# Attention's written order set by a count of TensorE's own columns instead of a count of calls

## The chip, the cores and the metric

The kernel runs on one core of one Trainium2 chip. The metric is the device time of one execution in microseconds (us), and a kernel's time is the median over its runs.

## What is computed

One inference step of a hybrid decoder layer, for a prompt of 1024 tokens and for 8 sample sequences of 4 tokens each, with a past of 8192 tokens in a paged cache. In the reference, cut to what matters here:

```python
h = rmsnorm(x, g_norm1) * (1 + scale1) + shift1      # shift, scale, gate = silu(c) @ w_ada + b_ada
za, zq, zkv, zg, zm = jnp.split(h @ w_in, SPLIT_IDX, axis=-1)
ya = chunk_spatial_gating(u, vn, w_spatial, b_spatial)
o = g[:, :, 0] * o_cmp + g[:, :, 1] * o_sel + g[:, :, 2] * o_win      # compressed, selected, window
mixed = (gate_a * (ya @ w_branch_a) + gate_b * (yb @ w_branch_b)) @ w_out
x = x + gate1 * mixed
x = x + gate2 * ((gelu(a) * gv) @ w_down)             # a, gv: causal convolution of h2 @ w_up
```

Attention has three branches per query: compressed blocks of 64 keys, a choice of 16 such blocks, and a window of 512 keys. For the prompt 16 blocks are all there are, so the choice takes everything; for the samples the kernel reads all selected-branch pages and masks those not chosen.

## The kernel before, in words

Activations lie transposed, features on the partitions and 1056 columns (1024 prompt, 32 sample) beside them. The stages follow each other: projections and compression of the paged cache, attention (about 612 to 1008 us of the span), the two branch products, the output product, the two feed-forward products.

In the attention three kinds of work share the engines:

- 32 **attention units** of the prompt: 8 tiles of 128 queries, in the order TILES, by 4 pairs of heads (`units`). `scores` puts a unit's products into PSUM, VectorE takes the negative maximum (L1134) and ScalarE the exponentials (L1135). `turn` transposes the probabilities on TensorE (L1160) and copies them back (L1164); `norm` and `values` finish the unit. `step(n)` writes the scores of unit n beside the transposes of unit n-1 and the values of unit n-2.
- 32 **sample units**: 8 sequences by 4 quarters of their pages. `sel_scores(m)` loads 16 pages of 128 KB (psel, issued by `load_pages` on SP's queue: a register load at L512 for every four pages, the DMAs at L522), multiplies them with the queries, adds the mask (L980) and takes the exponentials (L983). `sel_turn` transposes these (L990, copied back at L991); `sel_values` multiplies them with the pages' values (its copy is L1009). `sel_step(m)` writes the values of unit m-1 and then the scores of unit m, 33 steps in all.
- **Chains** of short steps with waits between them, Python generators in `pending`: `qtile` (a tile's compressed branch), `blocks`, `sel_merge` (joins four sample units), `near_turning` and `near_values` (window branch of the samples), `ada_late` (eight loads of w_ada, 2 MB each, L1052, and their products), `turning` (which calls `sel_turn`).

TensorE's order in this stage is the order in which the code writes its instructions (`manual_schedule` for PE); the other engines' order is made by a scheduler. The code decides in two ways. `due` gives for each unit n how many sample steps are to be written by its end, in proportion to the units' work (`work`), and `step` spreads those over its rounds (`at`). And `one_more`, called once or twice a round, lowers each chain's counter by one and runs a chain's next piece when the counter reaches 0: `later(turning(), 3)` is due at the third call. Where a piece is needed and has not been written, `sel_step` and `step` call `one_more` until it has.

The pages go through four buffers in turn (`page_buffer`): sample pages, window loads, w_ada loads, and at the end `ya` and `w_ba` (`ya_load`, L1261 and L1266). A load may start when the buffer's use four loads earlier is over, and the queue issues in order. Behind the attention `branch_a` multiplies `ya`, which `ya_split` splits into two parts, with `w_ba`.

Of the kernel before, what the change touches and what calls it, by code (L numbers as in the profile page):

```python
# [20 lines left out]
NEG = -1e30  # L21
AHEAD = 2
S2, S3 = 4, 2
EARLY = 8
# [26 lines left out]
def step_kernel(tc, A):  # L51
    nc = tc.nc
    sync, act, dve, pool, pe = nc.sync, nc.scalar, nc.vector, nc.gpsimd, nc.tensor

    def mm(out, lhsT, rhs, start, stop):
        return pe.matmul(out, lhsT, rhs, start=start, stop=stop)  # L56

    def behind(ins):
# [693 lines left out]
    def blocks(gr, bank):  # L752
# [21 lines left out]
        dve.tensor_scalar(p, p, r, None, op0=OP.mult)  # L774
        yield 3
        pt = bank()
# [19 lines left out]
        act.copy(pct, pt[:, 0:128])  # L796
        yield 6
        pt = bank()
# [9 lines left out]
        dve.tensor_scalar(oc, po[:, 0:128], GR[:, gr, 0:1], None, op0=OP.mult)  # L808
        yield 2
        pt = bank()  # L810
# [119 lines left out]
    def near_turn(gr):  # L930
        use, wv, s = near[gr]
        pst = R3([128, 640], F32, "pst", 2)
        pt = pM()
        for k in range(4):
            pe.transpose(pt[:, 128 * k:128 * k + 128], s[:, 128 * k:128 * k + 128], ident)
        act.copy(pst[:, 0:512], pt)
        pt = pM()
        pe.transpose(pt[0:32, 0:128], s[:, 512:544], ident)
        pool.memset(pst[:, 512:640], 0.0)
        dve.tensor_copy(pst[0:32, 512:640], pt[0:32, 0:128])  # L940
        near[gr] = use, wv, pst

    def near_values(gr):
        use, wv, pst = near.pop(gr)
        po = pM()
        for k in range(4):
            for i in range(4):
                mm(po[32 * i:32 * i + 32, 0:128], pst[:, 128 * k + 32 * i:128 * k + 32 * i + 32], wv[:, i, k], k == 0, False)
        for i in range(4):
            mm(po[32 * i:32 * i + 32, 0:128], pst[:, 512 + 32 * i:544 + 32 * i], vs_new[:, 128:256], False, True)  # L950
        ow = R3([128, 128], F32, "ou", 7)
        uses[use] = act.copy(ow, po[:, 0:128])
        yield 2
# [32 lines left out]
    def sel_turn(n, s):  # L986
        pst = R3([128, 640], F32, "pst", 2)
        pt = pM()
        for k in range(4):
            pe.transpose(pt[:, 128 * k:128 * k + 128], s[:, 128 * k:128 * k + 128], ident)  # L990
        dve.tensor_copy(pst[:, 0:512], pt)  # L991
        if n % 4 == 0:
            pt = pM()
            pe.transpose(pt[0:32, 0:128], s[:, 512:544], ident)
# [17 lines left out]
    def sel_merge(b):  # L1012
# [5 lines left out]
        dve.tensor_scalar(n4, cg4, nl, None, op0=OP.mult)  # L1018
        yield 3
        pt = pM()  # L1020
# [8 lines left out]
        dve.tensor_reduce(su, sf, axis=AX.X, op=OP.add)  # L1029
        yield 5  # L1030
        pt = pM()
# [6 lines left out]
        for i in range(1, 4):  # L1038
            dve.scalar_tensor_tensor(o, outs[i], f[:, i:i + 1], o, op0=OP.mult, op1=OP.add)
        yield 5  # L1040
        pt = pM()
# [22 lines left out]
    def qtile(i):  # L1064

        tile_of[i] = [q_first if i == TILES[0] else queries(i, KL[1][0]), None]
        yield 1
        c0 = 128 * i
# [18 lines left out]
        dve.tensor_tensor(s, s, z[:, :, None].to_broadcast([128, 8, 16]), op=OP.mult)  # L1087
        yield 8
        pt = pM()
        pe.transpose(pt[:, 0:128], s.rearrange("p a n -> p (a n)"), ident)  # L1090
        ct = R3([128, 128], F32, "ct", 2)
# [55 lines left out]
    def turn(n):  # L1147
# [6 lines left out]
        def group(parts):  # L1154

            pt = pM()
            c = 0
            for branch, h, k, w in parts:
                for b in range(k, k + w):
                    pe.transpose(pt[:, c:c + 128], probs[branch, h][:, 128 * b:128 * b + 128], ident)  # L1160
# [33 lines left out]
    def values(n):  # L1194
# [4 lines left out]
        for branch in range(2):  # L1199
            pe.transpose(pf[:, 128 * branch:128 * branch + 128], f[:, 128 * branch:128 * branch + 128], ident)  # L1200
        fs = R3([128, 256], F32, "fs", 2)
# [15 lines left out]
    def later(steps, wait):  # L1217

        pending.append([wait, steps])

    def one_more():

        for p in list(pending):
            p[0] -= 1
            if p[0] <= 0:
                wait = next(p[1], None)
                if wait is None:
                    pending.remove(p)
                else:
                    p[0] = wait  # L1230

    held, turned = {}, {}

    def sel_step(m):

        if m:
            while m - 1 not in turned:
                one_more()
            use, st, _ = held.pop(m - 1)
            sel_values(m - 1, use, st, turned.pop(m - 1))  # L1240
            if m % 4 == 0:
                later(sel_merge(m // 4 - 1), 2)
        if m < 32:
# [35 lines left out]
    def step(n):  # L1279

        nonlocal m, wba
        ds, gs = attend(n), turn(n - 1)
        if n % 4 == 2 and n + 2 < len(units):
            later(qtile(units[n + 2][0]), 1)
        if ds:
            ds.pop(0)()
        one_more()
        if n >= 2:
            while tile_of[units[n - 2][0]][1] is None:
                one_more()  # L1290
            values(n - 2)
        if gs:
            norm(n - 1)
        mine = list(range(m, due[n]))
        m = max(m, due[n])
        if n in (2, 6):
            near_scores(n // 4)
            later(near_turning(n // 4), 3)
# [5 lines left out]
        assert len(at) == len(mine)  # L1304
        if n % 4 == 1 and n < 32:
            later(ada_late(), 2)
        if n >= len(units):
            for j in range(4)[2 * (n - len(units)):2 * (n - len(units)) + 2]:
                ya_split(j)
        for r in range(rounds):  # L1310
            if r in at:
                sel_step(at[r])
            for _ in range(2):
                if gs:
                    gs.pop(0)()
            one_more()
            if ds:
                ds.pop(0)()
                one_more()
        if n == 0:  # L1320
            later(blocks(1, pM), 1)
        if n == len(units) - 1:
# [3 lines left out]
    with tc.manual_schedule(engines={mybir.EngineType.PE}):  # L1326
        later(qtile(TILES[0]), 0)
        one_more()
        for n in range(len(units) + AHEAD):
            step(n)  # L1330
        ma = []

# [16 lines left out]
        while pending:  # L1349
            one_more()  # L1350
    psum.release()
# [518 lines left out]
```

## Time and profile before

| | |
|---|---|
| median of 3 runs | 1973.37 us (1971.01 to 1976.99) |
| profiled execution | 1970.11 us, span 1968.4 us |
| PE busy | 1853.3 us, 94% of the span |
| PEld (weight loads) busy | 1744.9 us, 89% |
| DVE busy | 1178.6 us, 60% |
| ACT busy | 791.3 us, 40% |
| POOL busy | 486.7 us, 25% |
| moved by DMA | 345.09 MB, mean 175 GB/s |

The profile is of one execution; times in it are from the span's start. PE is TensorE's matmuls, PEld its weight loads, DVE VectorE, ACT ScalarE, POOL GpSimd, SP the engine that issues most DMAs; SPq is its queue. A wait row names the waiting instruction's line, what ended the wait, the total in us, how often, and the longest. In a timeline row the square brackets hold the idle time ahead and what ended it. Almost all matmuls have one line, L56, that of the helper `mm`, so they are told apart by their shapes and neighbours.

### The profile page before, as it was taken

What the parts mean: (1) busy time and instruction counts of PE and PEld (TensorE: products, weight loads), DVE (VectorE), ACT (ScalarE), POOL (GpSimd) and SP (SyncE); (2) the same over time, 40 slices, a digit from 0 to 9 for tenths busy, and PEclk for the clock granted to TensorE, in tenths of its full rate; (3) what the DMA queues carried; (4) which work ended last, traced back from release to release, by engine and by line L of the source; (5) the groups of instructions that cost most, each with busy time, mean ns of one, the idle gap of its engine ahead of it and who ended that gap; (6) DMA issues with size and microseconds to landing.
All of it is one profiled execution on the core that took longest, in us unless ns stands there. A gap on an engine that the chain in (4) does not pass through costs nothing.

```text
span 1968.4 us, 43754 instructions
## 1 busy us (share of the span) xinstructions
PE 1853.3 (94%) x16073; PEld 1744.9 (89%) x16073; DVE 1178.6 (60%) x2532; ACT 791.3 (40%) x1606; POOL 486.7 (25%) x624
## 2 busy tenths in 40 slices
PE   6799999999999998988999999799999999999996
PEld 4799999999997776767679999799999999999996
DVE  5713421112116666675565678899999999756464
ACT  4313111212115554655642366333444444545342
POOL 2510110000001000000002412756867765201010
PEclk9799999999999998999999999899999999999998
DMA  9274656776657777776774454233322223866463
GB/s 328 87 218 126 188 184 211 235 229 208 201 178 247 243 225 233 225 227 218 231 253 154 141 166 135 81 102 107 109 89 72 74 87 95 291 190 211 136 190 89
DMA packets 253607, 345.09 MB, mean 175 GB/s; under 512 B 35249, under 2 KB 189265, under 8 KB 251217
## 3 DMA queue, kind: packets, MB, share of 16 engines
q1 hardware_dynamic: 205408, 261.86, 42.4%
q10 hardware_dynamic: 36896, 41.22, 6.7%
q0 software_dynamic: 11088, 39.21, 5.6%
q8 instruction: 127, 2.08, 0.4%
q14 instruction: 88, 0.71, 0.1%
HBM read 304.91 MB, written 41.43 MB: 176 GB/s over the span
## 4 chain that ended last, share of the span: by engine, by line
PE 80%; DVE 5%; DMA 5%; SPq 4%; issue 3%; ACT 3%; POOL 1%; DVEq 0%; ACTq 0%; POOLq 0%
PE t L56 77%; SPq L522 3%; DMA t<-w_ada 2%; PE t L1160 2%; DVE t L320 1%; DMA t<-t 1%; DMA t<-psel 1%; POOL t L1553 1%; ACT t L319 1%; PE t L990 1%; DVE t L1590 1%; DVE t L1134 0%; SPq L512 0%; DVE t L338 0%; ACT t L1135 0%
## 5 line engine op out<-in xcount | busy, mean ns | idle before, releaser
L56 PE MATMUL t<-t,t 128*128 128x264 f32 (+12 forms) x15298 | 1775.9, 305 | 85.1 <-DVE t L173 14.8
L56 PEld LDWEIGHTS t<-t,t 128*128 128x128 f32 (+3 forms) x15138 | 1661.6, 170 | 135.8 <-issue 51.4
L320 DVE TENSOR_TENSOR t<-t,t 128x512 fp32r<-128x512 f32 (+2 forms) x478 | 386.4, 816 | 320.0 <-ACT t L319 315.9
L319 ACT CAST t<-t 128x512 fp32r<-128x512 f32 (+5 forms) x544 | 311.1, 589 | 440.7 <-PE t L56 342.6
L1590 DVE TENSOR_TENSOR t<-t,t 128x264 f32<-128x264 f32 (+2 forms) x366 | 107.2, 339 | 12.4 <-PE t L56 12.3
L1160 PEld LDWEIGHTS t<-t,t 128*128 128x128 f32 x528 | 58.5, 145 | 32.2 <-issue 13.3
L1191 POOL COPY t<-t 128x256 f32<-128x256 f32 x32 | 13.0, 407 | 279.8 <-DVE t L1189 176.9
L1528 ACT ACTIVATE t<-t,t 128x1072 f32<-128x1072 f32 x44 | 56.6, 1286 | 57.0 <-DVE t L1590 38.2
L1164 ACT COPY t<-t 128x512 f32<-128x512 f32 (+1 forms) x112 | 58.7, 569 | 49.0 <-PE t L1160 48.8
L683 ACT ACTIVATE t<-t 128x384 f32<-128x384 f32 (+1 forms) x48 | 22.2, 465 | 135.8 <-PE t L56 79.6
L1529 DVE SCALAR_TENSOR_TENSOR t<-t,t,t 128x1072 f32<-128x1072 f32 x44 | 73.1, 1661 | 5.0 <-ACT t L1528 4.5
L1160 PE MATMUL t<-t,t 128*128 128x128 f32 x528 | 75.2, 282 | 0.7 <-DVE t L1212 0.3
L1713 POOL TENSOR_TENSOR t<-t,t 128x384 f32<-128x384 f32 (+1 forms) x12 | 14.9, 1275 | 227.9 <-ACT t L1771 227.9
L1135 ACT ACTIVATE t<-t,t 128x640 f32<-128x640 f32 (+3 forms) x64 | 56.1, 877 | 35.7 <-DVE t L1134 31.1
L1530 DVE SCALAR_TENSOR_TENSOR t<-t,t,t 128x1072 f32<-128x1072 f32 x44 | 69.7, 1585 | 0.0
L1553 POOL TENSOR_TENSOR t<-t,t 128x512 f32<-128x512 f32 x22 | 46.6, 2117 | 89.6 <-DMA t<-w_up 79.0
L685 POOL DMA_DIRECT2D t<-t x16 | 8.5, 533 | 241.6 <-DVE t L684 186.8
L1134 DVE TENSOR_REDUCE t<-t 128x1 f32<-128x640 f32 (+3 forms) x64 | 58.9, 921 | 15.3 <-PE t L56 13.9
L1615 POOL TENSOR_TENSOR t<-t,t 128x1024 f32<-128x1024 f32 x22 | 53.8, 2446 | 17.1 <-ACT t L1614 17.1
L980 DVE TENSOR_TENSOR t<-t,t 128x512 f32<-128x512 f32 x32 | 22.1, 691 | 45.0 <-PE t L56 44.9
L1409 POOL TENSOR_TENSOR t<-t,t 128x384 f32<-128x384 f32 (+1 forms) x24 | 28.0, 1168 | 69.2 <-DVE t L1408 66.0
L320 DVE TENSOR_TENSOR t<-t 128x384 fp32r<-128x384 f32 (+1 forms) x66 | 37.0, 586 | 12.9 <-ACT t L319 12.8
(282 smaller groups left out, 1280.3 us busy)
## 6 DMA issues: line engine op xcount, KB each, us to landing
t<-psel SPq DMA_DIRECT2D x512, 128.0 KB
t<-pcmp SPq DMA_DIRECT2D x332, 128.0 KB
t<-w_down SPq DMA_DIRECT2D x120, 256.0 KB
t<-t POOLq DMA_DIRECT2D x50, 528.0 KB, 4.5
t<-w_up SPq DMA_DIRECT2D x96, 256.0 KB
t<-pcmp ACTq DMA_DIRECT2D x180, 128.0 KB
t<-w_ada SPq DMA_DIRECT2D x16, 1024.0 KB
t<-w_t ACTq DMA_DIRECT2D x52, 256.0 KB
```

Of the source, the lines that this page charges most:

```text
L56: return pe.matmul(out, lhsT, rhs, start=start, stop=stop)
L319: act.copy(hi, t)
L320: dve.tensor_tensor(lo, t, hi.bitcast(F32), op=OP.subtract)
L522: d = queue.dma_start(dst, src[bass.ds(r, 1)].rearrange("g p c -> p (g c)"))
L1134: dve.tensor_reduce(m4[:, branch, h:h + 1], ps[:, :, 0:w], axis=AX.XY, op=OP.max, negate=True)
L1160: pe.transpose(pt[:, c:c + 128], probs[branch, h][:, 128 * b:128 * b + 128], ident)
L1164: (act.copy if w > 2 else dve.tensor_copy)(probs[branch, h][:, 128 * k:128 * (k + w)], pt[:, c:c + 128 * w])
L1528: act.activation(acc[:, 0:w], up[:, 0:w], AF.Identity, scale=cw[:, n, 0:1], bias=cw[:, n, 3:4])
L1529: dve.scalar_tensor_tensor(acc[:, 0:w], up[:, 1:1 + w], cw[:, n, 1:2], acc[:, 0:w], op0=OP.mult, op1=OP.add)
L1530: dve.scalar_tensor_tensor(acc[:, 0:w], up[:, 2:2 + w], cw[:, n, 2:3], acc[:, 0:w], op0=OP.mult, op1=OP.add)
L1553: pool.tensor_tensor(s1, a21, a22, op=OP.add)
L1590: dve.tensor_tensor(o, by4(banks[c][:, c0:c0 + n], n), other(c, c0, n) if other else o, op=OP.add)
```

## The change

Counters of calls become counts of columns. `mm` and the new helper `turned_by` add to `spent` what each product costs in columns: its moving columns, four times those (times its share of 128 weight columns) where the weights are plain fp32, and 240 for a transpose. `later` and the new `advance` store for each chain the count at which its next piece is due, and `one_more` runs those whose count is reached. The waits are given as multiples of US = 2265 columns (4 for a sample unit's transposes; before, three calls). `due`, `work` and `at` go; instead a sample step is begun, at the next point where `deal` is called, when `spent` has passed `begin + m * every`, with `every` = 1504 times the units' work over 32, and 6400: 19,278 columns. `deal` is called twice a round. Where a piece is needed and not yet due, `hurry` runs the chain that is due next, whatever its count. Steps not begun by the end of the units are written behind them. No arithmetic changes.

```diff
@@ new names, and what is counted
+US = 2265
+    spent = [0]
     def mm(out, lhsT, rhs, start, stop):
+        m, n = lhsT.shape[-1], rhs.shape[-1] if len(rhs.shape) == 2 else rhs.shape[-1] * rhs.shape[-2]
+        spent[0] += n * m * 4 / 128 if lhsT.dtype == F32 else n
         return pe.matmul(out, lhsT, rhs, start=start, stop=stop)
+    def turned_by(out, x):
+        spent[0] += 240
+        return pe.transpose(out, x, ident)
@@ one of the waits in a chain (sel_merge)
-        yield 3
+        yield US * 3
@@ chains
-        pending.append([wait, steps])
+        pending.append([spent[0] + wait, steps])
+    def advance(p):
+        wait = next(p[1], None)
+        if wait is None:
+            pending.remove(p)
+        else:
+            p[0] = spent[0] + wait
     def one_more():
         for p in list(pending):
-            p[0] -= 1
-            if p[0] <= 0:
...
+            if p[0] <= spent[0]:
+                advance(p)
+    def deal():
+        nonlocal m
+        one_more()
+        if begin is not None and m < 33 and spent[0] >= begin + m * every:
+            m += 1
+            sel_step(m - 1)
+    def hurry():
+        advance(min(pending, key=lambda p: p[0]))
@@ sel_step
             while m - 1 not in turned:
-                one_more()
+                hurry()
...
-            later(turning(), 3)
+            later(turning(), US * 4)
-    work = [i + 1 + min(i + 1, 5) + 1 for i, _ in units]
-    due = [max(0, 33 * sum(work[2:n + 1]) // sum(work[2:])) for n in range(len(units))] + [33] * (AHEAD + 1)
-    m = 0
+    UNIT, SEL = 1504, 6400
+    every = UNIT * sum(i + 2 + min(i + 1, 5) for i, _ in units[2:]) // 32 + SEL
+    begin, m = None, 0
@@ step
-        mine = list(range(m, due[n]))
-        m = max(m, due[n])
+        if n == 2:
+            begin = spent[0]
-        at = {rounds * q // len(mine): k for q, k in enumerate(mine)}
         for r in range(rounds):
-            if r in at:
-                sel_step(at[r])
+            deal()
             for _ in range(2):
                 if gs:
                     gs.pop(0)()
-            one_more()
+            deal()
             if ds:
                 ds.pop(0)()
-                one_more()
@@ behind the units
+        while m < 33:
+            m += 1
+            sel_step(m - 1)
```

On TensorE, where the scores of sample unit 31 stand, the last of the pages' products (its four products of 32x512; the 32x128 x16 are the values of the sample unit before it, the 64x128 those of an attention unit, the 128x128 from t_69 transposes). Before:

```order
L1200 MATMUL t_13964<-t_69,t_13816 128x128 x2
L56 MATMUL t_13963<-t_13542,t_1481 128x128
L56 MATMUL t_13963<-t_13589,t_7377 64x128 x8
L56 MATMUL t_13963<-t_13745,t_7377 64x128 x8
L56 MATMUL t_13994<-t_13837,t_13943 32x128 x16
L56 MATMUL t_14067<-t_14013,t_3372 32x512 x4
L1160 MATMUL t_14075<-t_69,t_13783 128x128 x4
L1160 MATMUL t_14081<-t_69,t_13783 128x128 x4
L56 MATMUL t_14087<-t_7357,t_13057 128x512
```

In the changed kernel (its line 61 is `mm`, its line 65 `turned_by`):

```order
L65 MATMUL t_13912<-t_69,t_13814 128x128 x4
L61 MATMUL t_13918<-t_13761,t_13911 32x128 x16
L61 MATMUL t_13991<-t_13937,t_3372 32x512 x4
L65 MATMUL t_13999<-t_69,t_13681 128x128 x4
L65 MATMUL t_14005<-t_69,t_13681 128x128 x4
L61 MATMUL t_14011<-t_7357,t_13229 128x512
L61 MATMUL t_14011<-t_7359,t_13229 128x512
L61 LDWEIGHTS t_72
```

The scores of unit 31 stand one attention unit's work earlier: between them and the first product of `branch_a` lie 28 rows before and 51 now. The transposes of unit 30 now stand right ahead of their values.

On TensorE, the values of the second window load, near_values(1) (32x128 x16 from t_8878, then x4 from t_490). Before:

```order
L56 MATMUL t_9144<-t_84,t_8143 128x32
L56 MATMUL t_9147<-t_8878,t_9046 32x128 x16
L56 MATMUL t_9147<-t_490,t_9046 32x128 x4
L56 MATMUL t_9170<-t_8924,t_9057 32x128 x16
L56 MATMUL t_9243<-t_9189,t_3372 32x512 x4
L1160 MATMUL t_9251<-t_69,t_8820 128x128 x4
```

In the changed kernel:

```order
L65 MATMUL t_9233<-t_69,t_9124 128x128 x4
L61 MATMUL t_9239<-t_8878,t_9034 32x128 x16
L61 MATMUL t_9239<-t_490,t_9034 32x128 x4
L61 MATMUL t_9262<-t_9071,t_9232 32x128 x16
L61 MATMUL t_9335<-t_9281,t_3372 32x512 x4
L65 MATMUL t_9343<-t_69,t_8799 128x128 x4
```

Before, the values of sample unit 5 and the scores of unit 6 follow near_values(1); now those of units 6 and 7 do, and the earlier pair stands ahead of it.

On SP's queue, from the last pages of sample unit 30 to the first of unit 31 (each page is an ISA row, which sets the address, and a DMA; t_2558 is ya). Before:

```order
L522 ISA
L522 DMA t_13837<-psel 128x256
L1261 DMA t_14139<-t_2558 128x2x1056
L512 TENSOR_LOAD t_443
L522 ISA
L522 DMA t_14013<-psel 128x256
```

In the changed kernel:

```order
L531 ISA
L531 DMA t_13761<-psel 128x256
L521 TENSOR_LOAD t_443
L531 ISA
L531 DMA t_13937<-psel 128x256
```

The first half of ya's load stood between the two units' pages; now it stands behind those of unit 31, next to the second half.

More of the change, by code (lines that the diff above doesn't have):

```diff
@@ L796, in blocks @@
         act.copy(pct, pt[:, 0:128])
-        yield 6
+        yield US * 8
         pt = bank()
@@ L934, in near_turn @@
         for k in range(4):
-            pe.transpose(pt[:, 128 * k:128 * k + 128], s[:, 128 * k:128 * k + 128], ident)
+            turned_by(pt[:, 128 * k:128 * k + 128], s[:, 128 * k:128 * k + 128])
         act.copy(pst[:, 0:512], pt)
         pt = pM()
-        pe.transpose(pt[0:32, 0:128], s[:, 512:544], ident)
+        turned_by(pt[0:32, 0:128], s[:, 512:544])
         pool.memset(pst[:, 512:640], 0.0)
@@ L989, in sel_turn @@
         for k in range(4):
-            pe.transpose(pt[:, 128 * k:128 * k + 128], s[:, 128 * k:128 * k + 128], ident)
+            turned_by(pt[:, 128 * k:128 * k + 128], s[:, 128 * k:128 * k + 128])
         dve.tensor_copy(pst[:, 0:512], pt)
@@ L993, in sel_turn @@
             pt = pM()
-            pe.transpose(pt[0:32, 0:128], s[:, 512:544], ident)
+            turned_by(pt[0:32, 0:128], s[:, 512:544])
             pool.memset(pst[:, 512:544], 0.0)
@@ L1087, in qtile @@
         dve.tensor_tensor(s, s, z[:, :, None].to_broadcast([128, 8, 16]), op=OP.mult)
-        yield 8
+        yield US * 7
         pt = pM()
-        pe.transpose(pt[:, 0:128], s.rearrange("p a n -> p (a n)"), ident)
+        turned_by(pt[:, 0:128], s.rearrange("p a n -> p (a n)"))
         ct = R3([128, 128], F32, "ct", 2)
@@ L1159, in group @@
                 for b in range(k, k + w):
-                    pe.transpose(pt[:, c:c + 128], probs[branch, h][:, 128 * b:128 * b + 128], ident)
+                    turned_by(pt[:, c:c + 128], probs[branch, h][:, 128 * b:128 * b + 128])
                     c += 128
@@ L1199, in values @@
         for branch in range(2):
-            pe.transpose(pf[:, 128 * branch:128 * branch + 128], f[:, 128 * branch:128 * branch + 128], ident)
+            turned_by(pf[:, 128 * branch:128 * branch + 128], f[:, 128 * branch:128 * branch + 128])
         fs = R3([128, 256], F32, "fs", 2)
@@ L1241, in sel_step @@
             if m % 4 == 0:
-                later(sel_merge(m // 4 - 1), 2)
+                later(sel_merge(m // 4 - 1), US * 2.5)
         if m < 32:
@@ L1279, in step @@
     def step(n):
-        nonlocal m, wba
+        nonlocal begin, wba
         ds, gs = attend(n), turn(n - 1)
         if n % 4 == 2 and n + 2 < len(units):
-            later(qtile(units[n + 2][0]), 1)
+            later(qtile(units[n + 2][0]), 0)
         if ds:
@@ L1293, in step @@
             norm(n - 1)
-        mine = list(range(m, due[n]))
-        m = max(m, due[n])
+        if n == 2:
+            begin = spent[0]
         if n in (2, 6):
             near_scores(n // 4)
-            later(near_turning(n // 4), 3)
+            later(near_turning(n // 4), US * 4.5)
         if n in (3, 7):
@@ L1302, in step @@
         rounds = max((len(gs) + 1) // 2, len(ds), 1)
-        at = {rounds * q // len(mine): k for q, k in enumerate(mine)}
-        assert len(at) == len(mine)
         if n % 4 == 1 and n < 32:
-            later(ada_late(), 2)
+            later(ada_late(), US * 2.5)
         if n >= len(units):
@@ L1315, in step @@
                     gs.pop(0)()
-            one_more()
+            deal()
             if ds:
                 ds.pop(0)()
-                one_more()
         if n == 0:
-            later(blocks(1, pM), 1)
+            later(blocks(1, pM), 0)
         if n == len(units) - 1:
@@ L1349, in step_kernel @@
         while pending:
-            one_more()
+            hurry()
     psum.release()
```

18 lines of the change are left out of this document (7 added, 11 removed).

## The prediction

> **What bounds the kernel now.** I read the page first, for the span, and then the table of stages, because only the attention's written order changes.
>
> ```profile
> span 1968.4 us, 43754 instructions
> 612.00:681.00 69.00, 61.49 (x759) 47.55 (x756) 45.56 (x130) 39.63 (x96) 4.01 (x11) 1.00 0.81 250
> 681.00:993.00 312.00, 285.55 (x3325) 219.15 (x3318) 202.99 (x549) 176.31 (x481) 22.52 (x58) 0.96 0.73 228
> 993.00:1008.00 15.00, 12.70 (x156) 9.38 (x156) 10.28 (x18) 11.27 (x24) 2.43 (x4) 1.00 0.68 230
> 1008.00:1020.00 12.00, 10.13 (x81) 9.61 (x82) 9.63 (x34) 4.17 (x10) 1.20 (x2) 1.00 0.84 316
> 760.00:778.00 18.00, 12.46 (x89) 8.36 (x93) 7.07 (x14) 5.46 (x14) 0.52 (x2) 0.62 0.68 208
> ```
>
> The columns are the stretch, its length, the busy time of PE, PEld, DVE, ACT and POOL, the granted clock, the DMA share and GB/s. The attention runs from about 612 to 1008 us. In its long middle PE is idle for 312 - 285.55 = 26.5 us, and a clock of 0.96 costs another 0.04 x 312 = 12.5 us. So at most some 40 us could be won there. The next question is what PE waits for in that middle, and what SP's queue (which issues the sample pages) waits for.
>
> ```profile
> PE t L56 <- DMA t<-psel: 9.5, 3, 4.5
> PE t L990 <- ACT t L983: 9.5, 10, 2.5
> PE t L56 <- DVE t L991: 2.8, 4, 1.1
> SPq L522 <- DMA t<-w_ada: 16.4, 12, 2.6
> SPq L522 <- PE t L56: 4.9, 8, 2.9
> SPq L522 <- DMA t<-t: 0.4, 1, 0.4
> ```
>
> The figures are total, times and longest. PE has two large waits: for the pages of a sample unit (three times), and for the exponentials that the sample unit's transposes at L990 read (ten times). The change aims at the second kind. The first decides more, and the queue's own timeline shows why:
>
> ```profile
> 664.07 9.83 SPq L522 DMA_DIRECT2D t<-psel  x16
> 673.99 0.39 SPq L908 DMA_DIRECT2D t<-wk  x1
> 674.43 3.25 SPq L910 DMA_DIRECT2D t<-wv  x4
> 681.12 41.67 SPq L522 DMA_DIRECT2D t<-psel  x64
> 722.88 2.35 SPq L1052 DMA_DIRECT2D t<-w_ada  x2
> 725.82 23.38 SPq L522 DMA_DIRECT2D t<-psel  x32
> 749.30 0.85 SPq L1052 DMA_DIRECT2D t<-w_ada  x2
> 750.74 64.31 SPq L522 DMA_DIRECT2D t<-psel  x96
> ...
> 947.03 34.35 SPq L522 DMA_DIRECT2D t<-psel  x48
> 981.48 0.38 SPq L1261 DMA_DIRECT2D t<-t  x1
> 982.47 10.08 SPq L522 DMA_DIRECT2D t<-psel  x16
> 992.64 0.39 SPq L1261 DMA_DIRECT2D t<-t  x1
> ```
>
> Each row is start, length and count; 16 pages are one sample unit. From 681.12 to 992.55 the pages of units 5 to 31 follow each other with no gap above some 0.6 us: 27 units in 311.4 us, 11.5 us a unit. The queue hardly ever waits there for PE to free a buffer (4.9 us, the longest time 2.9, in the gap before 681.12). So the queue sets when each unit's pages are there, and PE follows it. The end of the attention shows both:
>
> ```profile
> 985.76 1.09 PE L1160 MATMUL t<-t,t 128*128 128x128 f32 x8
> 986.61 1.54 PE L56 MATMUL t<-t,t 128*128 128x512 f32 x8
> 988.01 1.07 PE L1160 MATMUL t<-t,t 128*128 128x128 f32 x8
> 988.92 0.60 PE L990 MATMUL t<-t,t 128*128 128x128 f32 x4
> 989.27 1.36 PE L56 MATMUL t<-t,t 128*128 128x512 f32 x6
> 990.48 0.39 PE L1200 MATMUL t<-t,t 128*128 128x128 f32 x2
> 990.70 3.29 PE L56 MATMUL t<-t,t 128*128 128x128 f32 x66
> 994.54 1.29 PE L56 MATMUL t<-t,t 128*32 128x512 f32 x8 [0.55 <-DMA t<-psel]
> ...
> 1000.00 1.08 PE L56 MATMUL t<-t,t 128*32 128x128 f32 x32 [0.99 <-DVE t L991]
> ...
> 1008.17 4.16 PE L56 MATMUL t<-t,t 128*128 128x128 f32 x43 [0.55 <-DVE t L1023]
> ```
>
> The scores of unit 31 (994.54) wait 0.55 us for pages whose last issue ended at 992.55, and 13.6 us pass on PE before the next stage's matmuls (1008.17). Here TensorE and the queue arrive together.
>
> **The change part by part.** No engine gets more or less work; only the order changes, PE's by hand and that of the others after it.
>
> *The transposes of a sample unit.* They now come due after US*4 = 9060 columns instead of three calls. Counted by the change's own rule over both orders, they stood 1536 to 7984 columns behind their scores, 13 of 32 under 4500; now none is under 4788. So most of the 9.5 us at L990 goes. Against that, values follow their transposes at once 14 times instead of 5 (sample steps that force a transpose, or find it just made). Such a pair costs up to the 0.99 us of the row at 1000.00; 9 more are up to 9 us, at the least 9 x 2.8/4 = 6 us by the waits for L991. The two nearly cancel, and neither decides if PE then meets the queue anyway: what PE saves it waits for at the next pages. I count them at nothing; uncovered, they are -9.5 + 6 to 9 us.
>
> *The sample steps earlier.* No step stands more than 512 columns later than before, and most stand far ahead. Unit 31's scores begin at column 632,828 of 671,596 instead of 646,236. Its pages do not come earlier for that: the queue is the same 32 units, eight w_ada loads and two window loads. So 13,408 columns that PE did while the pages came are now done behind them. In the order these are one attention unit's 16 transposes, its scores and its values: the rows from 985.76 to 993.99, 8.23 us, less the sample transposes (next start 989.27 - 988.92 = 0.35) and 16 sample value products (1.08). That is **+6.8 us**. The rate of the whole stage gives 13,408 / (671,596 / 359.74 us) = 7.2 us, from this row:
>
> ```profile
> 612.00:1008.00 396.00, 359.74 (x4223) 276.08 (x4219) 258.83 (x697) 227.21 (x600) 28.96 (x72) 0.97 0.74 232
> ```
>
> *When the queue ends.* First, the load of ya at 981.48 moves behind unit 31's pages: its 0.38 us, the 0.1 us ahead of it, and the 0.4 us that a page waits for it go, **-0.9** (-0.4 to -1.2). Second, unit 8's pages take the buffer of the second window load, which is free after near_values(1):
>
> ```profile
> 710.20 0.27 ACT L952 COPY t<-t 128x128 f32<-128x128 f32 x1 [2.12 <-PE t L56]
> 713.66 9.13 SPq L522 DMA_DIRECT2D t<-psel  x16
> ```
>
> Those products move behind the values of unit 5 and the scores of unit 6, from column 164,292 to 169,588: 5296 columns, 2.8 us at the stage's rate. 710.47 + 2.8 = 713.3, and the queue came to unit 8 at 713.66: **0**. The bounds are -1 (unit 5's buffer is free sooner, as PE waits less before 681) and +2 (the forced pair just ahead costs its full wait twice). The w_ada loads stand up to two units later between the pages; the 16.4 us of waits behind them stay.
>
> *Behind the attention.* PE's 12 - 10.13 = 1.9 us of idle from 1008 to 1020, and the 0.55 at 1008.17, come while the branch's operands are loaded and split. These now have 6 us more: **-1.2**, between -2.4 and 0.
>
> *The clock.* PE now idles more in the middle, by those 6.8 us. What clustered waits do is in the row 760 to 778: 0.62 granted, 18 x 0.38 = 6.8 us of TensorE lost. A stretch in the middle is paid out of the waits for pages; one near units 30 or 31 is not. I take a quarter of that loss there, **+1.7** (0 to half of it, +3.4).
>
> The Trainium skill (TensorE: Matmul & The Clock Gate, "HAM oscillation — how this bites in real kernels") warns of idle gaps above about 3.4 us; by that alone only a wait like the longest one here, 4.5 us, would halve the clock; this term would be 0 and the sum 4.7. The trace does not bear that out: 12.46 of the 18 us to 778 were busy, and the clock fell there.
>
> Sum: 6.8 - 0.9 + 0 - 1.2 + 1.7 = **+6.4 us**; the ends are 6.8 - 1.2 - 1 - 2.4 + 0 = +2.2 and 7.2 - 0.4 + 2 + 3.4 = +12.2. The profiled execution took 1970.1 us (span 1968.4 and 1.7 around it), so 1976.5; the median of the three runs, 1973.4, is 3.3 us above it, so I forecast **1980** (1976 to 1986).
>
> **Rivals.**
> *PE is the bound (faster).* If the queue has slack and unit 31's pages are issued by 985 or sooner, the shorter waits are won: -9.5 at L990, -6.8 of lost clock, +6 for new pairs, some -10 us: 1963. For it: DMA is busy only 0.73. Against: the queue's rows without gaps, and the 0.55 us at 994.54. The Trainium skill (DMA: Bandwidth & Descriptors, "Specifications") gives 358 GB/s for a core, an estimate of 0.64 of that being used at 228 GB/s; by it the transfers have room, and only the issuing would be the limit.
> *The queue gets shorter (no change).* If the later, wider spaced w_ada loads meet the pages better and a third of the 16.4 us goes, -5.5: +1.5, 1975. For it: one load now falls inside unit 20's pages. Against: eight loads still share the lanes with the pages.
> *The forced pairs are not covered (slower still).* If PE comes late to each page because of them, their 9 us add to the sum less what PE waited: up to +13, 1986.
> That the order does not change is no rival: PE's order is written by hand, and it differs.
>
> **How the numbers follow.** About 0.3%, 5.9 us, is what a measurement of this kernel can tell from no change. My sum lies just above it, so its case, 0.55, is split: 0.45 over that, 0.10 under. The forced pairs have 0.05, all over. The shorter queue has 0.20, all within. The faster rival has 0.20. That makes 0.20 faster, 0.30 the same, 0.50 slower. The range runs from 1967, where half of the faster rival is left out, to 1987, the upper end of the sum and a little of the forced pairs.
>
> **What would show it.** Right: in the changed trace the pages of units 8 to 31 again follow without a gap and end within 2 us of 992; PE's waits for L983 fall below 3 us while its waits for psel rise to 15 us or more; the scores of unit 31 wait for pages; about 20 us of PE work follow them, and the next stage begins near 1014. Wrong: the last page is issued by 987 or earlier; or PE's waits for psel do not rise; or SP waits for PE in the middle (buffers), which would be the forced pairs; or the attention ends before 1008.

## The result and the profile after

The changed kernel took 1981.69 us (median of 9 runs, 1978.56 to 1993.57), the kernel before 1971.42 us beside it (median of 9, 1964.54 to 1976.99). The ratio is 1.0064, 95% interval 1.0038 to 1.0089: slower by 7 to 18 us. The medians lie 10.3 us apart. A second set of runs gave 1.0061 (1.0040 to 1.0082). The forecast was +6.4 us and 1980 us.

First the span from the profile's page, and the table of stages of the changed kernel, with the columns as in the prediction (stretch, length, busy time of PE, PEld, DVE, ACT and POOL, granted clock, DMA share, GB/s).

```profile
span 1977.0 us, 43742 instructions
```

```profile
681.00:993.00 312.00, 277.79 (x3223) 209.84 (x3222) 199.41 (x542) 169.40 (x466) 21.13 (x55) 0.97 0.73 225
993.00:1008.00 15.00, 13.80 (x172) 10.49 (x174) 7.56 (x14) 8.52 (x22) 1.31 (x3) 1.00 0.72 279
1008.00:1020.00 12.00, 9.20 (x95) 7.65 (x92) 9.04 (x23) 11.09 (x22) 2.64 (x3) 0.96 0.05 7
612.00:1008.00 396.00, 355.39 (x4165) 269.45 (x4165) 253.15 (x688) 217.69 (x586) 26.65 (x70) 0.97 0.74 230
```

In the same 312 us of the middle PE is busy 277.79 us instead of 285.55: 34.2 us idle instead of 26.5. The last row shows 4.4 us less of PE's busy time by 1008, and from 1008 to 1020 there is hardly any DMA (0.05 busy, 0.84 before): the attention now goes on in that stretch. Aligned on PE's last products ahead of the attention, which come 1.4 us earlier in this execution ("aligned", from here on), the products behind the attention start 6.95 us later than before. Further on, in stages that the change does not touch, this execution loses 3.0 us more. Of the twelve other traces of this study eight are 2.9 to 7.2 us later there as well, of kernels whose ratios go from 0.9992 to 1.0061, so I do not count that part to the change.

The waits from 681 to 993, PE's first and then SP's queue (total, times, longest). L1000 is VectorE's copy of the transposed exponentials, L992 is the exponential.

```profile
PE t L61 <- DVE t L1000: 14.3, 13, 3.2
PE t L61 <- DMA t<-psel: 8.3, 3, 3.3
...
PE t L65 <- ACT t L992: 0.9, 1, 0.9
SPq L531 <- DMA t<-w_ada: 15.8, 10, 3.2
SPq L531 <- PE t L61: 6.3, 5, 5.0
```

The wait that the change aims at is gone: 0.9 us instead of 9.5. In its place stands the wait for the turned tiles, 14.3 us instead of 2.8. The waits for pages are a little smaller, 8.3 instead of 9.5, and all three lie ahead of 760. The w_ada waits are 15.8 instead of 16.4. SP has one new long wait for PE, 5.0 us.

SP's queue, where it reaches unit 5 and where it ends (start, length, count):

```profile
661.36 12.04 SPq L531 DMA_DIRECT2D t<-psel  x16
673.50 0.39 SPq L917 DMA_DIRECT2D t<-wk  x1
673.94 2.97 SPq L919 DMA_DIRECT2D t<-wv  x4
678.18 57.91 SPq L531 DMA_DIRECT2D t<-psel  x80
736.19 0.86 SPq L1061 DMA_DIRECT2D t<-w_ada  x2
...
922.28 44.65 SPq L531 DMA_DIRECT2D t<-psel  x64
967.03 0.85 SPq L1061 DMA_DIRECT2D t<-w_ada  x2
968.48 22.82 SPq L531 DMA_DIRECT2D t<-psel  x32
991.39 0.89 SPq L1285 DMA_DIRECT2D t<-t  x2
```

Unit 5's pages begin at 678.18, 1.6 us sooner than before once the 1.4 us are allowed for: the gaps ahead of units 3 to 5 shrank from 13.1 to 7.3 us together, and some of it went into a slower issue of unit 4 (12.04 us, 9.83 before). But the five units from 678.18 take 57.91 us, where before four took 41.67, 10.4 a unit: 5.8 us too many. Most of them are SP's 5.0 us wait, which lies ahead of unit 8; its pages begin 4.4 us later than before when aligned. At the end all is level again: the last page is issued by 991.30, and 992.55 before, 0.1 us apart when aligned. From unit 8 on the gaps between units came to 18.9 us instead of 21.7, and the issue of the pages to 255.7 instead of 257.2. ya's two halves now stand together behind it.

PE between unit 5's values and near_values(1) (in brackets the idle time ahead and what ended it):

```profile
698.42 0.66 PE L65 MATMUL t<-t,t 128*128 128x128 f32 x4 [0.87 <-ACT t L992]
699.96 1.08 PE L61 MATMUL t<-t,t 128*32 128x128 f32 x32 [0.88 <-DVE t L1000]
704.35 1.83 PE L61 MATMUL t<-t,t 128*32 128x512 f32 x8 [3.31 <-DMA t<-psel]
...
715.57 3.03 PE L61 MATMUL t<-t,t 128*32 128x128 f32 x80
```

ACT's copy of near_values(1), which frees unit 8's buffer:

```profile
716.94 0.27 ACT L961 COPY t<-t 128x128 f32<-128x128 f32 x1 [2.80 <-PE t L61]
```

Here is the pair (698.42, 699.96), then a wait of 3.31 us for unit 6's pages, whose products now stand ahead of near_values(1). The copy that came at 710.20 before comes at 716.94, 8.1 us later when aligned.

The end of the attention on PE. The row x40 holds unit 30's values (32 records) and unit 31's scores (8); 128x384 are the branch's products. The row in the second block is of before.

```profile
991.97 0.65 PE L65 MATMUL t<-t,t 128*128 128x128 f32 x4
993.41 1.94 PE L61 MATMUL t<-t,t 128*32 128x128 f32 x40 [0.79 <-DVE t L1000]
...
1003.23 1.08 PE L61 MATMUL t<-t,t 128*32 128x128 f32 x32 [0.78 <-DVE t L1000]
...
1012.65 2.38 PE L61 MATMUL t<-t,t 128*128 128x128 f32 x34
1016.55 0.45 PE L61 MATMUL t<-t,t 128*128 128x384 f32 x1 [1.51 <-ACT t L328]
1017.58 0.44 PE L61 MATMUL t<-t,t 128*128 128x384 f32 x1 [0.58 <-DVE t L329]
1018.38 11.91 PE L61 MATMUL t<-t,t 128*128 128x384 f32 x62 [0.36 <-DVE t L1361]
```

```profile
1018.47 13.81 PE L56 MATMUL t<-t,t 128*128 128x32 f32 x75 [1.70 <-DVE t L1039]
```

Unit 31's scores begin at 994.31, 0.90 us into the row at 993.41, and 22.24 us pass until the branch's first product. This stretch is called the tail from here on. Before, the scores began at 994.54. The row at 1008.17, which I took for the next stage, begins with the 34 value products of the last attention unit, so the branch's first product came at 1010.49, 15.95 us behind the scores. The tail is 6.29 us longer. That is most of the 6.95; another 1.0 us lies between the last page and the scores (3.01 instead of 1.99 us), where unit 30's pair waits 0.79.

### The profile page after: what moved, and what is told of

It is laid out like the page before. It is cut to its first block, busy times and chain, and to the rows that moved or that the text cites. A ratio compares the mean times of both kernels' runs of the same rounds, so it can differ in the third digit from the quotient of the medians.

```text
span 1977.0 us, 43742 instructions
## 1 busy us (share of the span) xinstructions
PE 1855.6 (94%) x16073; PEld 1742.8 (88%) x16073; DVE 1175.6 (59%) x2532; ACT 789.1 (40%) x1606; POOL 485.6 (25%) x624
## 4 chain that ended last, share of the span: by engine, by line
PE 79%; DVE 7%; DMA 5%; ACT 3%; issue 2%; SPq 2%; POOL 1%; DVEq 0%; ACTq 0%; POOLq 0%
PE t L61 76%; PE t L65 3%; DMA t<-w_ada 2%; DVE t L329 1%; SPq L531 1%; DMA t<-t 1%; POOL t L1576 1%; ACT t L1144 1%; DMA t<-w_down 1%; ACT t L328 1%; DVE t L1143 1%; DMA t<-psel 1%; DVE t L1613 0%; DVE t L347 0%; ACT t L1173 0%
## 5 line engine op out<-in xcount | busy, mean ns | idle before, releaser
L61 PE MATMUL t<-t,t 128*128 128x264 f32 (+13 forms) x15298 | 1779.5, 306 | 98.5 <-DVE t L1000 17.0
L65 PEld LDWEIGHTS t<-t,t 128*128 128x128 f32 x746 | 81.9, 144 | 35.5 <-issue 15.6
L65 PE MATMUL t<-t,t 128*128 128x128 f32 x746 | 108.3, 280 | 5.1 <-DVE t L1096 2.7
L1552 DVE SCALAR_TENSOR_TENSOR t<-t,t,t 128x1072 f32<-128x1072 f32 x44 | 71.5, 1624 | 11.6 <-ACT t L1551 10.9
L1553 DVE SCALAR_TENSOR_TENSOR t<-t,t,t 128x1072 f32<-128x1072 f32 x44 | 66.5, 1511 | 0.0
L1144 ACT ACTIVATE t<-t,t 128x640 f32<-128x640 f32 (+3 forms) x64 | 56.2, 879 | 21.2 <-DVE t L1143 18.9
L329 DVE TENSOR_TENSOR t<-t 128x384 fp32r<-128x384 f32 (+1 forms) x66 | 37.1, 586 | 13.4 <-ACT t L328 13.1
```

The source lines that it names most:

```text
L65: return pe.transpose(out, x, ident)
L329: dve.tensor_tensor(lo, t, hi.bitcast(F32), op=OP.subtract)
L1144: act.activation(P[:, 0:L].rearrange("p (a c) -> p a c", a=2), ps[:, :, 0:w], AF.Exp, bias=m4[:, branch, h:h + 1], accum_out=s4[:, branch, ...
L1552: dve.scalar_tensor_tensor(acc[:, 0:w], up[:, 1:1 + w], cw[:, n, 1:2], acc[:, 0:w], op0=OP.mult, op1=OP.add)
L1553: dve.scalar_tensor_tensor(acc[:, 0:w], up[:, 2:2 + w], cw[:, n, 2:3], acc[:, 0:w], op0=OP.mult, op1=OP.add)
```

## The experiments

All but the first row are timed in five rounds, four kernels to a set, beside the kernel before on the same chip. "Column" is where unit 31's scores start in TensorE's column count from the attention's start (before: 646,236, changed: 632,828); "pairs" are sample units whose values follow their transposes at once (5 and 14).

| kernel | column | pairs | ratio to before (95%) |
|---|---|---|---|
| changed | 632,828 | 14 | 1.0064 (1.0038 to 1.0089) |
| changed_again | 632,828 | 14 | 1.0061 (1.0040 to 1.0082) |
| unit5_first | 632,828 | 14 | 1.0042 (1.0028 to 1.0056) |
| turn_sooner | 632,828 | 3 | 1.0031 (1.0014 to 1.0049) |
| steps_alone | 632,700 | 4 | 1.0030 (1.0015 to 1.0045) |
| before_early | 632,700 | 5 | 1.0080 (1.0061 to 1.0099) |
| steps_wider | 646,364 | 16 | 0.9994 (0.9979 to 1.0010) |
| both | 646,364 | 1 | 0.9997 (0.9984 to 1.0011) |
| waits_alone | 646,364 | 22 | 1.0009 (0.9995 to 1.0023) |
| waits_alone2 | 646,364 | 5 | 0.9992 (0.9975 to 1.0009) |
| both_wider | 657,596 | 3 | 1.0034 (1.0019 to 1.0048) |

Two runs with a second queue for the pages, further below, are not in the table. The theory is that of the prediction: the page queue ends when it ends, and what TensorE has left to do behind unit 31's pages is what is paid. The chief rival is that the pairs cost their waits by themselves.

**steps_wider: the sample steps later, the pairs kept.**

```
-    every = UNIT * sum(i + 2 + min(i + 1, 5) for i, _ in units[2:]) // 32 + SEL
+    every = UNIT * sum(i + 2 + min(i + 1, 5) for i, _ in units[2:]) // 32 + SEL + 450
```

> The changed kernel with sample steps 450 columns further apart, so that unit 31's scores stand at column 646,364 as before, with 16 forced pairs instead of 14. My theory: the 13,500 columns come back ahead of unit 31's pages, and the time falls by 6 to 7 us against the changed kernel, to within 3 us of before; PE waits for pages as little as before. Rival (pairs): as the changed kernel or slower, 7 to 10 us above before.

Measured: 0.9994 (0.9979 to 1.0010). PE's waits from 681 to 993:

```profile
PE t L61 <- DVE t L1000: 13.8, 14, 1.7
...
PE t L61 <- DMA t<-psel: 3.1, 3, 1.2
```

The end of its queue on SP:

```profile
980.19 10.73 SPq L531 DMA_DIRECT2D t<-psel  x16
```

The end of its attention on PE:

```profile
994.25 1.44 PE L61 MATMUL t<-t,t 128*32 128x512 f32 x8 [0.43 <-ACT t L1018]
...
1007.90 0.44 PE L61 MATMUL t<-t,t 128*128 128x384 f32 x1 [0.35 <-ACT t L328]
```

This execution reaches the attention 1.1 us sooner than before, the changed one 1.4, so the two can be set side by side to some 0.3 us. The last page is issued by 990.92 (991.30 in the changed kernel), the scores of unit 31 begin at 994.25 (994.31), and then 13.65 us pass instead of 22.24. The pairs' wait is nearly as long as there, 13.8 us, and costs nothing that the ratio shows: the waits for pages fell to 3.1. Behind the attention the two executions are 10.3 us apart, and 8.6 of them are the tail. By the ratios the kernels differ by some 14 us, where the theory gave 6 to 7; the rest is not shown to be the tail's.

**turn_sooner: the pairs gone, the sample steps kept.**

```
-            later(turning(), US * 4)
+            later(turning(), US * 2)
```

> The changed kernel with a sample unit's transposes due after 2 x 2265 columns instead of 4 x 2265. Unit 31's scores stay at column 632,828; values that follow their transposes at once fall from 14 to 3. My theory (the end is set by the page queue and by the work behind unit 31's pages): PE's waits for the copied transposes (14.3 us in the changed profile) go, but its waits for pages take their place; unit 31's scores move up by at most 1 us, and the attention ends within 1 us of the changed kernel's; time 6 to 9 us above before. Rival (the forced pairs are what costs): the attention ends 7 us or more sooner than in the changed kernel; time at or under before's.

Measured: 1.0031 (1.0014 to 1.0049). Still slower than before with 3 pairs instead of 14, so the pairs are not the whole cause; the interval overlaps the changed kernel's. In its profiled execution, though, the products behind the attention start only 0.4 us later than before, 6.5 us sooner than in the changed kernel: my theory allowed 1 us and the rival asked for 7, so by this sign the theory failed. The order differs in a second thing, which I had not seen: unit 5's pages find their buffer ahead of the second window load, and unit 8's do not wait for near_values(1). The last page is issued by 987.40, 3.3 us sooner than in the changed kernel when aligned. This run alone can't tell the pairs from the buffer.

```profile
964.26 23.14 SPq L531 DMA_DIRECT2D t<-psel  x32
```

**both: turn_sooner and steps_wider together.**

> Both edits together: steps 450 columns further apart and transposes due after 2 x 2265 columns; unit 31's scores at column 646,364, one pair. My theory: unit 31's pages and 25,000 columns behind them set the end, as before: 1 to 4 us under before at best, since the first half of ya's load is no longer ahead of the pages. Rival (pairs): as turn_sooner, since the pairs are gone in both; 10 us or more under before if PE alone is the bound.

Measured: 0.9997 (0.9984 to 1.0011). One pair instead of 16 gives nothing against steps_wider: PE waits 1.0 us for L1000, 12.8 less, but 10.3 us for pages, 7.2 more, and 5.8 us for the exponentials, where steps_wider had no such wait. What is saved at the pairs is waited for there.

**before_early: the kernel before, with each sample unit from the eighth one attention unit sooner.**

```
+    due = [due[n + 1] if 8 <= n < len(units) else due[n] for n in range(len(due))]
```

A second edit lets a round hold several sample steps, which the moved table needs.

> The kernel before, its counts of calls kept, with the due table read one attention unit ahead from unit 8 on: unit 31's scores at column 632,700 as in the changed kernel, 5 pairs as before. My theory: slower than before by 6 to 8 us, as the changed kernel, though no pair was added; PE's waits for pages rise. Rival (pairs): within 2 us of before.

Measured: 1.0080 (1.0061 to 1.0099). Without any of the change's counts, the earlier order alone is slower, and by more than the work behind unit 31. The queue's waits and its end show one reason:

```profile
SPq L522 <- PE t L56: 14.6, 7, 8.8
```

```profile
973.22 23.45 SPq L522 DMA_DIRECT2D t<-psel  x32
```

The queue now waits 14.6 us for PE to free buffers, 8.8 of them ahead of unit 19, and its last page is issued by 996.67, 6.8 us later than before when aligned. By calls, the steps move by whole attention units, and some come in bunches. The tail is 23.3 us, and PE's waits for pages rose to 16.1 as expected. The direction is the theory's; the size is made of two things and does not measure the tail.

**both_wider: +800 instead of +450, with US*2.**

> As both, with the steps 800 instead of 450 columns further apart: unit 31's scores at column 657,596, 11,200 columns later still, three pairs. My theory: PE's waits for pages shrink to under 5 us, 14,000 columns stay behind unit 31's pages, and the time falls by 3 to 6 us against both. Rival (PE itself is the bound by then, or the chain behind unit 31 comes too late for the next stage): no faster than both, or slower by up to 5 us.

Measured: 1.0034 (1.0019 to 1.0048). I expected it faster, and that failed: SP waits 17.6 us for buffers, the last page is issued 12.0 us later than in before when aligned, and the 5.6 us that are saved in the tail (10.3 us) are more than lost ahead of it. A likely reason is that a later step holds the buffer of the unit ahead of it longer, and so the queue. Of the three places tried, 646,000 is the best; where between 633,000 and 657,000 the best one lies is not shown.

**two_queues and both_two_queues: one of four page groups issued by ScalarE's queue, in the changed kernel and in `both`.**

```
-                   after, (), 3)
+                   after, (3, 7), 3)
```

> The changed kernel with one in four groups of four sample pages issued from ACT's queue instead of SP's; order on TensorE as in the changed kernel. My theory (queue and tail): the pages of unit 31 are there some 8 us or more sooner, PE no longer waits for pages (8.3 us in the changed profile between 681 and 993) and the time falls by 4 to 8 us against the changed kernel, to within 5 us of before; the rest, 14 us at the pairs, stays. Rival (transfers, not issuing, set the pace): the pages come no sooner, the waits behind w_ada grow, time within 2 us of the changed kernel.

> The kernel of the run both (steps 450 columns further apart, transposes due after 2 x 2265 columns) with one in four groups of pages from ACT's queue. My theory: its waits for pages (10.3 us between 681 and 993) go, and it falls 6 to 10 us under both and before. Rival (transfers set the pace, or ACT is held up by its own loads): within 3 us of before, or slower.

Measured: 1.0145 (1.0119 to 1.0172) and 1.0024 (1.0007 to 1.0041). Neither is faster than the kernel that it was to speed up. A wait of ScalarE's in two_queues, from 676 to 1010, and one of PE's, from 681 to 993:

```profile
ACT t L992 <- DMA t<-psel: 16.6, 4, 6.9
```

```profile
PE t L61 <- ACT t L1144: 10.5, 10, 5.4
```

and a place where its own work stands behind its page loads:

```profile
876.23 0.27 ACT L1018 COPY t<-t 128x128 f32<-128x128 f32 x1 [3.68 <-PE t L61]
876.80 2.18 ACTq L531 DMA_DIRECT2D t<-psel  x4
879.46 0.72 ACT L992 ACTIVATE t<-t,t 128x512 f32<-128x512 f32 x1 [2.97 <-DMA t<-psel]
```

ScalarE first copies a sample unit's values (876.23), then issues four pages (2.18 us), and only then comes the exponential. The changed kernel has no such wait at L992; PE's wait for the exponentials of the attention units (L1144) was 5.0 us there and is 10.5 here. In two_queues the last page is issued 13.4 us later than in the changed kernel when aligned, where I expected 8 sooner; in both_two_queues it is issued 3.2 us sooner than in both, but unit 31's scores begin 1.4 us later. As a test of a shorter queue both runs are inconclusive: they put a new wait into ScalarE. The Trainium skill (Trainium Kernel Development and Optimization, "Key Constraints") says that issuing from several engines only saves the sequencer's issue time. These runs agree in so far as there was issue time to save (PE's waits for pages fell from 8.3 to 2.0 us, and in the second from 10.3 to none), and show what it cost here.

**steps_alone: steps by columns, the waits of the chains by calls as before.** The links keep before's counts, and only the sample steps go by columns. Against the changed kernel:

```
-        yield US * 6
+        yield 3
...
-        pending.append([spent[0] + wait, steps])
+        pending.append([wait, steps])
```

> One half of the change alone: sample steps at even shares of columns, all chain waits by calls as before. Unit 31's scores at column 632,700, 4 pairs. My theory: 4 to 8 us above before, like turn_sooner (1.0031). Rival (the pairs alone cost): within 2 us of before.

Measured: 1.0030 (1.0015 to 1.0045). The step half of the change, with fewer pairs than before, is slower. In its profiled execution the last page is issued 2.4 us sooner than in before when aligned, and the tail is 21.4 us instead of 15.95. Here too unit 5's pages come ahead of the second window load and unit 8's do not wait for it.

**waits_alone and waits_alone2: the other half.** Links by columns, sample steps by before's table of calls; waits_alone2 has the transposes due after US*2 as well.

```
-        if begin is not None and m < 33 and spent[0] >= begin + m * every:
...
+        mine = list(range(m, due[n]))
+        m = max(m, due[n])
```

> The other half of the change alone: every link of a chain is due by columns (the sample transposes after US*4), the sample units are placed by before's table of calls. Unit 31 stands at column 646,364, as before; 22 sample units have their values right behind their transposes. Theory: with unit 31 where it was, 0.9975 to 1.002 of before; PE's waits for the exponentials go, waits for the turned tiles of about 20 us take their place and that of the waits for pages, the last page ends between 990 and 993. Rival (the pairs cost PE's time whatever the queue does): 22 pairs instead of 5, slower by over 0.5%, 1.005 or more.

> As waits_alone, with the sample transposes due after US*2: unit 31 at column 646,364, 5 pairs. Theory (the queue is the bound): 0.998 to 1.001, what PE saves at the exponentials and the pairs it waits for at the pages. Rival (PE's own waits are the bound): clearly under waits_alone and under before, 0.996 or less.

Measured: 1.0009 (0.9995 to 1.0023) and 0.9992 (0.9975 to 1.0009). PE's waits in waits_alone, 681 to 995:

```profile
PE t L61 <- DVE t L1000: 18.3, 19, 2.0
```

With 22 pairs and 18.3 us of waits at them PE waits for no page at all, and the time is that of before. With 5 pairs it waits 7.0 us for pages and 2.4 at the pairs, and the time is the same again. The rival of the pairs asked for 1.005 or more in the first, and the rival of PE's own waits for 0.996 or less in the second; both are out for a unit 31 at this column.

**unit5_first and changed_again: the changed kernel without the wait ahead of unit 8, and as it is.**

```
-        if begin is not None and m < 33 and spent[0] >= begin + m * every:
+        if begin is not None and m < 33 and spent[0] >= begin + m * every - 4000 * (m == 5):
```

> The changed kernel, but sample unit 5 comes 4000 columns sooner, so that its pages take their buffer ahead of the second window load, and unit 8's pages no longer take the buffer that near_values(1) frees. Unit 31 stays at column 632,828 and the 14 pairs of transposes and values stay. Theory (the queue and the work behind unit 31's pages, with the 4.7 us ahead of unit 8's pages as a further part): the pages of unit 8 start near 714 instead of 718 by the time of before, the last page ends 2.5 to 3.5 us sooner, and the ratio to before falls from 1.0064 to about 1.0035. Rival (the 14 pairs cost their 14.3 us of waits by themselves): the last page is sooner, but PE takes no profit of it, and the ratio stays at 1.006 or more.

> The changed kernel once more, beside the three others on one chip, so that unit5_first is compared with it there. Theory: 1.004 to 1.008 of before, unit 8's pages again some 4 us late. Rival (the 1.0064 was the chip or the hour): within 1.003.

Measured: 1.0042 (1.0028 to 1.0056) and 1.0061 (1.0040 to 1.0082). SP's queue in unit5_first:

```profile
684.50 0.39 SPq L917 DMA_DIRECT2D t<-wk  x1
684.95 2.92 SPq L919 DMA_DIRECT2D t<-wv  x4
688.05 42.00 SPq L531 DMA_DIRECT2D t<-psel  x61
...
962.26 23.55 SPq L531 DMA_DIRECT2D t<-psel  x32
```

Pages now follow each other past unit 8 (61 in 42.00 us), and the last is issued by 985.81, 3.0 us sooner than in the changed kernel when aligned. The products behind the attention follow by 3.3 us. The time fell by less than can be told from nothing: the means of the runs are 1976.6 and 1979.5, 2.8 us apart with an uncertainty (one standard error) of 1.7. The repetition also shows how much the place varies: in its profiled execution the gap ahead of unit 8 is 2.2 us, its pages begin 1.7 us late and not the 4 that I expected, and the products behind the attention are 3.9 us late, not 6.95. So the buffer's wait costs 3.3 us in one pair of traces and 0.3 in the other, and by the times between nothing and 6.

**Together.** The four kernels at column 646,364 lie at 0.9998 on average, with 1, 5, 16 and 22 pairs. Those at 632,700 to 632,828 (without before_early) lie between 1.0030 and 1.0064. In their profiled executions the tail is 21.4 to 22.5 us, at 646,364 13.3 to 16.8 (before: 15.95). The products behind the attention start 0.4 to 6.95 us later than in before (mean 4.0), at 646,364 1.3 to 3.6 us sooner (mean -2.6): 6.6 us apart, where the prediction had 6.8 for the work moved behind the pages. That the second group lies ahead of before, at before's own column, no time shows. None of the kernels beats the one before by more than its interval.

The early group falls into two parts. The three in which unit 8's pages do not wait for near_values(1) are at 1.0030, 1.0031 and 1.0042, the two in which they do at 1.0061 and 1.0064. So the earlier place of the sample steps alone, with few pairs and no such wait, costs some 0.3%, 6 us. What adds the rest in the changed kernel, the buffer's wait or the 14 pairs, these runs do not separate. The clock is not the reason: stretches of half clock cost TensorE 6.8 us in the attention of steps_alone, which is 5.2 us late, and 10.2 in both, which is 3.6 us early.

## Why the prediction was right, and where its terms were not

**The bound: right.** Where unit 31 stands against the queue decides: at 646,364 four kernels with 1 to 22 pairs take the time of before, and at 632,700 to 632,828 all are slower, with 3 to 14 pairs. But "PE waits for the pages" was too simple. From 760 on PE in the changed kernel waits for no page. It arrives at unit 31 some 1.0 us late, by unit 30's pair, just when the queue has ended. So two of my signs of being wrong showed, though the bound held: PE's waits for psel did not rise to 15 us, they fell to 8.3, and unit 31's scores stand behind a wait for VectorE's copy and not for pages; and SP waited for PE in the middle, 5.0 us at once. I had put that second sign down to the forced pairs, but it stands at the second window load's buffer: unit5_first, with the same pairs, has no such wait above 1.6 us. My reading that the queue has "no gap above some 0.6 us" was wrong too: a row of its timeline runs on over waits, and inside the rows of before the queue stands still for up to 2.8 us behind a w_ada load.

**The work behind unit 31's pages, +6.8: right, and a little large.** The tail is 6.29 us longer, with 1.51 us of a wait for ScalarE's split in it (below). Without PE's waits (2.47 us in this tail, 1.87 before) it is 5.7 us longer. About 20 us were to follow the scores and 22.24 do; the 2 us are my reading of the row at 1008.17, where the next stage begins only behind 34 products. The term is a difference, and did not suffer.

**The transposes and the pairs, counted at nothing: mis-sized, and hidden for the most part.** The exponentials' wait fell as expected, 9.5 to 0.9. The pairs' wait rose by 11.5 us (2.8 to 14.3), not by 6 to 9; single ones took up to 3.2, since VectorE had other work ahead of the turned tile. "The two nearly cancel" was out by 3 us. The cover held where unit 31 was late (steps_wider, waits_alone). In the changed kernel it was just used up: 1.0 us came through at unit 30. Whether the 14 pairs cost more than that there is not settled; turn_sooner (1.0031) and unit5_first (1.0042) overlap.

**The queue's end, -0.9 and 0: the second failed.** ya's load moved as said. "710.47 + 2.8 = 713.3" left out what PE would wait for between the moved products: 2.8 us of columns, 3.31 us for unit 6's pages, and about 1.7 us for a stretch of half clock right behind that wait (below) are 7.8, and the copy came 8.1 us later. Unit 8's pages began 4.4 us late, where I had allowed +2. That the queue still ended level is because the 4.4 us that unit 8 was late were made up behind it, 2.8 in the gaps (the w_ada loads stand elsewhere, ya's no longer between pages) and 1.5 in the issue itself, where I had only ya's 0.9. Two errors cancelled. A product that is put behind another unit's pages takes over that unit's wait.

**Behind the attention, -1.2: not seen.** PE waits 1.51 for ScalarE's split, 0.58 and 0.36 for VectorE; before it was 1.70. The splits are ScalarE's and VectorE's work, and they moved back with the attention's own: ScalarE's first one begins at 1009.55 with no idle time ahead of it, where before it began at 1000.63. Of its 11.09 busy us from 1008 to 1020 some 7 are splits; before, the stretch held 4.17 in all.

**The clock, +1.7: not seen.** The middle's granted clock is 0.97 (0.96 before). The 0.96 from 1008 to 1020 is a stretch of half clock that begins at 1019.0; the trace of before has the same one, at 1019.9. There is no further dip in the tail.

**The sum.** Term by term the trace has 0.1 at the queue's end, 1.0 ahead of the scores, 6.3 in the tail, and -0.8 in the waits just behind it (0.94 instead of 1.70): 6.6 of the 6.95 us seen. That the forecast of +6.4 is near this is in part luck: -1.2 and +1.7 did not come, the -0.9 was used up by unit 8's lateness, and the 1.0 ahead of the scores was not in it. That 1980 is near 1981.69 is luck too, since the kernel before took 2 us less over these nine runs than over the three that I started from. The rivals: "PE is the bound" needed the last page by 985, and it came level; "the queue gets shorter" asked for a third of the w_ada waits, and 0.6 us went (2.8 of the gaps behind unit 8). What stays open is the rest of the ratio: 1.0064 is 12.6 us, twice the forecast, and the trace of one execution shows 7 at the attention, that of the repetition 4. The profiled execution, 1978.7 us, was 3 us under its median.

## What to carry to other kernels

Where a load queue runs through a stage without a gap, look at how much compute stands behind the last load: an order that starts each unit sooner brought the last data at most 3 us sooner here, and put some 6 us of other work behind them. The waits that TensorE showed in the middle were exchanged for one another (exponentials, turned tiles, pages), and where the last unit stood as before, removing one of them gave nothing. When work is moved past a wait, price it at the wait's length too, and ask which buffer its result frees.

## What the runs showed of the hardware

TensorE's clock fell to half for 3.4 us around short waits. Stretches of the changed kernel (columns as above):

```profile
700.00:705.00 5.00, 1.69 (x37) 1.09 (x40) 0.98 (x4) 0.27 (x1) 0.00 (x0) 1.00 0.65 186
705.00:708.40 3.40, 3.40 (x18) 2.29 (x11) 1.38 (x2) 0.81 (x2) 0.00 (x0) 0.50 0.71 204
899.50:902.90 3.40, 3.13 (x40) 1.78 (x40) 2.55 (x11) 0.57 (x2) 0.14 (x1) 0.50 0.71 220
```

```profile
701.54:704.96 3.42, 0.61 (x5) 0.32 (x8) 0.00 (x0) 0.00 (x0) 0.00 (x0) 1.00 0.59 163
896.10:899.52 3.42, 1.77 (x18) 1.58 (x14) 3.16 (x11) 1.62 (x6) 0.33 (x1) 1.00 0.69 203
```

The products at the start of the stretch from 899.50:

```profile
899.76 2.79 PE L61 MATMUL t<-t,t 128*32 128x128 f32 x36 [1.89 <-DVE t L1000]
```

From 705.0 the clock is 0.50 for 3.4 us, just behind the wait of 3.31 us at 704.35; from 899.5 it is 0.50 again, around a wait of only 1.89 us. Each such stretch takes 1.7 us of TensorE's work, nearly as much as the second wait itself. The Trainium skill (TensorE: Matmul & The Clock Gate, "HAM oscillation — how this bites in real kernels") speaks of idle gaps above about 3.4 us; both waits here are shorter, so the trace does not agree with that as a bound.

The length of the single wait is not what decides in this trace. Its seven stretches of half clock from 681 to 1023 begin at 704.96, 728.86, 752.75, 814.19, 861.98, 899.52 and 1018.99, all of them whole multiples of 3.413 us apart, and in the 3.4 us ahead of each TensorE was busy for only 0.61 to 1.87 us (the last two of the rows are two of these). Two other such windows, from 698.13 and 721.99, were busy for 1.74 and 1.85 us and no half clock followed, so near 1.8 us the trace shows both.
